# Seven block products for eight in nine more weight pairs, with one low part per pair made by an adding transfer

## The chip, the cores and the metric

The kernel runs on one core of a Trainium2 chip. A core has TensorE (PE in the profile; PEld is its weight load), VectorE (DVE), ScalarE (ACT), GpSimd (POOL) and SyncE (SP), an on-chip memory of 128 partitions, matrix accumulators in eight banks (PSUM), and 16 DMA engines that move data between HBM and the on-chip memory. The metric is the device time of one execution in microseconds.

## The reference

One encoder block over 256 positions of width 2048, in float32. What matters here are its five large matrix products: the input projection, the output projection `mix @ w_out` (2048 x 2048), the up product of the feed-forward part (2048 x 11264), its down product (5632 x 2048), and at the end a gate:

```
mix = jnp.concatenate([y_ssd, y_pool], axis=-1) @ w_out[i]
h = h + rmsnorm(mix, mix_norm_post[i])
hn = rmsnorm(h, ffn_norm_pre[i])
ff = conv_glu(hn, w_ffn_up[i], ffn_conv_w[i], ffn_conv_b[i], w_ffn_down[i])
h = h + rmsnorm(ff, ffn_norm_post[i])
gate = jax.nn.sigmoid(rmsnorm(h, ple_norm_pre[i]) @ w_ple_gate[i])
h = h + rmsnorm(gate * (p[i] @ w_ple[i]), ple_norm_post[i])
```

## The kernel before

**Products in three passes.** Every float32 operand is split into a high part, rounded to the format that PE multiplies in one pass, and a low part, the rest. A product is then three matmuls: high by high, high by low, low by high. `split` (L138) makes the two parts of a weight tile: ScalarE copies the tile with rounding (L147), VectorE subtracts the rounded copy from the tile (L148).

**Token-major products.** `token_major` (L240) computes 1024 columns of one product for both tiles of 128 positions. It is called twice per product, for half 0 and half 1 of the 2048 columns. The contraction runs over tiles of 128 (`k`), two at a time: a pair is one load of 2 x 128 rows by 1024 columns (1 MB, `raw`, L151, issued by SP, three buffers), and then the splits. The high and low parts live in five buffers each (tags `whi` and `wlo`), so a buffer is written again when PE has done with the tile five allocations before. A normal pair is 2 k x 2 position tiles x 2 column blocks x 3 passes = 24 matmuls of 128x512. In the last pair of a half the matmuls go bank by bank, so that the first banks can be emptied while the last are filled. In the second half of the gate the last four pairs go together in that way (`tail` is 4); eight of their tiles' high and low parts then have to be held at once, and two pairs get theirs in spare pages (`spare`, L136).

**Seven products for eight.** In the down product about one pair in three (`fast`) is not multiplied block by block. A pair is a 2 x 2 block product: two position tiles by two k tiles on one side, two k tiles by two column blocks on the other, eight block products. `seven_products` (L201) forms sums of the blocks on both sides and needs seven, 21 matmuls for 24. On the weight side VectorE makes the differences in place in the loaded pair (L209 to L211), and there are four splits: `a` (512 columns), `b`, `c` and `d` (1024 each). On the other side `hid_sums` (L800) makes four sums of 128x128 blocks, which are kept and used again in the second half. Four of the seven products go into accumulators of their own, and `combine` (L222) adds these to the four result banks after the last fast pair of the half, with VectorE, while the next pair runs.

**The order of the work.** The program's tile scheduler sets the order of each engine's queue when it is built; each engine then works through its queue in order and waits on semaphores. So an instruction that waits holds up everything behind it on its engine. In the output projection `sublayer` (L701) runs both halves, empties each bank with a square on ScalarE (L718) and a gain product on VectorE (L719), and then makes the next operand. The scan before it (`mix`, L604) ends in the same stretch of time as the projection begins, with additions on GpSimd (L612); the transposes of its result (`y_turn`, L686) run between pairs 2 and 4 of the projection. The gate's loop is at L864.

Of the kernel before, what the change touches and what calls it, by code (L numbers as in the profile page):

```python
# [16 lines left out]
P = 128  # L17
# [34 lines left out]
def build(nc, a, out):  # L52
# [5 lines left out]
    with tile.TileContext(nc) as tc, \  # L58
# [79 lines left out]
        def split(name, src, nel, cuts=()):  # L138
# [9 lines left out]
                last["dve"] = ins(nc.vector.tensor_sub(lo[:, s], src[:, s], hi[:, s].bitcast(F32)))  # L148
            return hi, lo

        def raw(name, src, a_, b_):  # L151
            r = wp.tile([P, 2048], F32, tag="raw", bufs=3, name=name)
            last["dma"] = load(r[:, :a_ * b_].rearrange("p (a b) -> p a b", a=a_), src, True)
            return r
# [43 lines left out]
                yield o, c  # L198
                c += o.shape[-1]

        def seven_products(name, r, a_, acc, alt, start, stop):  # L201

            v = r.rearrange("p (b c) -> p b c", b=4)
            b11 = split(f"{name}a", r[:, :512], 512)
            b2 = split(f"{name}b", r[:, 1024:], 1024)

            nc.vector.tensor_sub(v[:, 0:2], v[:, 1::2], v[:, 0:2])  # L209
            nc.vector.tensor_sub(v[:, 3], v[:, 3], v[:, 0])  # L210
            nc.vector.tensor_sub(v[:, 2], v[:, 2], v[:, 3])  # L211
# [10 lines left out]
        def combine(name, acc, alt):  # L222

            m = [mid(f"{name}v{i}") for i in range(2)]
            p1, s16, s165, s167 = (m[i // 2][:, i % 2 * 512:(i % 2 + 1) * 512] for i in range(4))

            def add(o, a_, b):
                nc.vector.tensor_add(o, a_, b)
# [11 lines left out]
        def token_major(name, w, c0, ks, get, acc, tail=1, fast=(), alt=None, sums=None):  # L240


            group, nu = [], len(ks) // 2
            for u in range(nu):
                k0 = ks[2 * u]
                r = raw(f"{name}r{k0}", w[k0 * P:(k0 + 2) * P, c0:c0 + 1024]
                        .rearrange("(k p) c -> p k c", p=P), 2, 1024)
                if u in fast:
                    seven_products(f"{name}{k0}", r, sums(k0), acc, alt, u == fast[0], u == fast[-1])
                    continue  # L250
                for j in range(2):
                    group.append((k0 + j, *split(f"{name}{k0}_{j}", r[:, j * 1024:(j + 1) * 1024], 1024)))
                if nu - tail <= u < nu - 1:
                    continue

                order = [(t, o, g, q) for t in range(2) for o in columns(acc[t]) for g in group for q in range(3)] \
                    if u == nu - 1 or u - 1 in fast[-1:] else \
                    [(t, o, g, q) for g in group for t in range(2) for q in range(3) for o in columns(acc[t])]
                for t, (o, c), (k, wh, wl), q in order:
                    xh, xl = (v[:, t * P:(t + 1) * P] for v in get(k))  # L260
                    xx, ww = ((xh, wh), (xh, wl), (xl, wh))[q]
                    mm(o, xx, ww[:, c:c + o.shape[-1]], k == ks[0] and q == 0, k == ks[-1] and q == 2)
                if u - 1 in fast[-1:]:
                    combine(name, acc, alt)
                group = []
                aside()

# [430 lines left out]
            load(g, src.partition_broadcast(P))  # L698
            return g

        def sublayer(name, w, ks, get, gain, h, vnext, panel=Panel, fast=((), ()), sums=None):  # L701

            mg = [page(f"{name}m{t}") for t in range(2)]
            sq = [[], []]
            for half in range(2):

                alt = main(f"{name}s{half}") if fast[half] and half == 0 else []
                acc = [main(f"{name}a{half}{t}") for t in range(2)]
                if fast[half]:
                    alt += (main(f"{name}s{half}") if half else []) + [misc(f"{name}s{half}_{i}") for i in (2, 3)]  # L710
                token_major(f"{name}{half}", w, half * 1024, ks, get, acc, 1, fast[half], alt, sums)
# [88 lines left out]
        def hid_sums(k):  # L800
# [3 lines left out]
            if k not in kept:  # L804
# [5 lines left out]
                s = mid(f"hd{k}")  # L810
                s1, s2, s3, s4 = (s[:, i * P:(i + 1) * P] for i in range(4))
                nc.vector.tensor_add(s1, a21, a22)
                nc.vector.tensor_sub(s3, a11, a21)
                nc.vector.tensor_sub(s2, s1, a11)
                nc.vector.tensor_sub(s4, a12, s2)
                o = keep[-1][:, n % 2 * 1024:(n % 2 + 1) * 1024] if n < 4 else mid(f"he{k}", F32R)
                nc.scalar.copy(o[:, :512], s[:, :512])
                nc.vector.tensor_sub(o[:, 512:], s[:, :512], o[:, :512].bitcast(F32))
                if n < 4:
                    kept[k] = o  # L820
            else:
                o = kept[k]
            d = {f"s{i + 1}": (o[:, i * P:(i + 1) * P], o[:, 512 + i * P:512 + (i + 1) * P]) for i in range(4)}
# [28 lines left out]
        def finish(t):  # L852
# [5 lines left out]
            for c in range(4):  # L858
# [2 lines left out]
                                               op0=ALU.mult, op1=ALU.add)  # L861
                nc.sync.dma_start(out[t * P:(t + 1) * P, s], vg[t][:, s])

        for half in range(2):  # L864
            acc = [main(f"gt{half}{t}") for t in range(2)]
            if half == 1:

                acc[1] = acc[1][:1] + [acc[1][1][:, :256], main("gtz")[0][:, :256]]

                for i in (8, 6):  # L870
                    sh, sl = page(f"gth{i}", F32R), page(f"gtl{i}", F32R)
                    for j in range(2):
                        spare[f"gt1{NK - i}_{j}"] = (sh[:, j * 1024:(j + 1) * 1024], sl[:, j * 1024:(j + 1) * 1024])
# [68 lines left out]
```

## Time and profile before

| what | us |
|---|---|
| median of 3 runs (1146.38 to 1147.10) | 1146.65 |
| the profiled execution | 1147.28 |
| its span | 1145.5 |
| PE busy in the span | 1126.3 |
| VectorE busy | 824.8 |
| ScalarE busy | 598.3 |
| GpSimd busy | 122.5 |

The profile is one execution. Busy time is the time in which an engine had an instruction at work; idle time of an engine that does not set the end costs nothing. The chain of work is followed back from the last instruction, at each step to what released it. PE's two edited stages are the output projection from 208.7 to 299.3 us and the gate product from 1042.4 to 1134.0 us of the span. A landing time of a transfer is from its issue to its semaphore.

### The profile page before, as it was taken

The page shows a single profiled execution, that of the slowest core. Times are in us where ns is not written, and L with a number is a line of the kernel's source. Part 1 is how long each engine was busy: PE and PEld are TensorE (multiplying, and loading weights), DVE is VectorE, ACT ScalarE, POOL GpSimd, SP SyncE. Part 2 cuts the span into 40 slices and gives each one's busy share as a digit, 9 for nine tenths or more (in the row PEclk, how much of TensorE's full clock was granted, in tenths as well). Part 3 has the DMA queues.
Part 4 walks back from the last instruction along what each step waited for, and adds up shares of the span by engine and source line. Part 5 has one row for each costly group of instructions (what it writes and reads, how often), then busy time and mean ns, then how long its engine had stood idle before and what let it go on. Part 6 is the DMA issues. An engine that isn't in the chain of part 4 may idle for free.

```text
span 1145.5 us, 15408 instructions
## 1 busy us (share of the span) xinstructions
PE 1126.3 (98%) x6057; PEld 971.6 (85%) x6057; DVE 824.8 (72%) x1060; ACT 598.3 (52%) x812; POOL 122.5 (11%) x123
## 2 busy tenths in 40 slices
PE   9998999999999999999999999999999999999996
PEld 9997987888888888888888888888888888887885
DVE  6578896654777665666766766668888888898573
ACT  7533543553675454544544545545555556657462
POOL 0274504200110000000000000000000000002001
PEclk9998999999999999999999999999999999999998
DMA  9952347546365555555555565556466646564752
GB/s 358 337 184 74 111 150 267 201 156 216 121 213 186 192 192 195 190 185 184 184 187 193 181 207 189 184 184 221 159 209 221 204 163 221 187 206 159 226 179 74
DMA packets 129592, 219.03 MB, mean 191 GB/s; under 512 B 3696, under 2 KB 96752, under 8 KB 128624
## 3 DMA queue, kind: packets, MB, share of 16 engines
q1 hardware_dynamic: 129232, 217.70, 57.4%
q8 instruction: 47, 0.77, 0.3%
q10 hardware_dynamic: 288, 0.36, 0.1%
q14 instruction: 25, 0.20, 0.1%
HBM read 215.95 MB, written 2.10 MB: 190 GB/s over the span
## 4 chain that ended last, share of the span: by engine, by line
PE 92%; DVE 5%; POOL 1%; ACT 1%; issue 1%; POOLq 0%; DVEq 0%; ACTq 0%
PE va L86 21%; PE ga L86 21%; PE dna L86 17%; PE woa L86 8%; PE gt L86 7%; PE dtu L86 4%; PE z L86 4%; PE xbc L86 3%; PE dns L86 3%; DVE cv L373 2%; DVE w L586 1%; DVE xb_0l L148 1%; PE ple L86 1%; PE yd L86 0%; DVE h L726 0%
## 5 line engine op out<-in xcount | busy, mean ns | idle before, releaser
L86 PE MATMUL ga<-wox,ug_0h 128*128 128x512 f32 x352 | 125.5, 395 | 0.0
L86 PE MATMUL ga<-wox,ug_1h 128*128 128x512 f32 x352 | 125.1, 394 | 0.0
L86 PE MATMUL va<-wox,uv_0h 128*128 128x512 f32 x352 | 124.8, 393 | 0.0
L86 PE MATMUL va<-wox,uv_1h 128*128 128x512 f32 x352 | 124.8, 393 | 0.0
L86 PE MATMUL ga<-wox,ug_0l 128*128 128x256 f32 x352 | 99.1, 282 | 0.0
L86 PE MATMUL ga<-wox,ug_1l 128*128 128x256 f32 x352 | 99.1, 282 | 0.0
L86 PE MATMUL va<-wox,uv_0l 128*128 128x256 f32 x352 | 99.1, 281 | 0.0
L86 PE MATMUL va<-wox,uv_1l 128*128 128x256 f32 x352 | 99.1, 281 | 0.0
L86 PEld LDWEIGHTS va<-wox,uv_0h 128*128 128x128 f32 x352 | 66.1, 188 | 15.0
L86 PEld LDWEIGHTS va<-wox,uv_1h 128*128 128x128 f32 x352 | 66.1, 188 | 15.0
L86 PEld LDWEIGHTS ga<-wox,ug_1h 128*128 128x128 f32 x352 | 66.1, 188 | 14.9
L86 PEld LDWEIGHTS ga<-wox,ug_0h 128*128 128x128 f32 x352 | 66.1, 188 | 14.8
L86 PE MATMUL dna<-dn_0h,hs 128*128 128x512 f32 x248 | 75.8, 393 | 0.0
L86 PE MATMUL dna<-dn_1h,hs 128*128 128x512 f32 x248 | 75.6, 393 | 0.0
L767 POOL TENSOR_TENSOR fc<-fc,rfb 128x1024 f32<-128x1024 f32 x11 | 26.4, 2404 | 440.2 <-ACT fc L766 440.2
L86 PEld LDWEIGHTS ga<-wox,ug_0l 128*128 128x128 f32 x352 | 66.2, 188 | 0.1
L86 PEld LDWEIGHTS ga<-wox,ug_1l 128*128 128x128 f32 x352 | 66.2, 188 | 0.0
L86 PEld LDWEIGHTS va<-wox,uv_0l 128*128 128x128 f32 x352 | 66.2, 188 | 0.0
L86 PEld LDWEIGHTS va<-wox,uv_1l 128*128 128x128 f32 x352 | 66.2, 188 | 0.0
L86 PEld LDWEIGHTS dna<-dn_1h,hs 128*128 128x128 f32 x248 | 46.5, 188 | 10.8
L86 PEld LDWEIGHTS dna<-dn_0h,hs 128*128 128x128 f32 x248 | 46.5, 188 | 10.7
L86 PE MATMUL dna<-dn_0l,hs 128*128 128x512 f32 x124 | 40.2, 393 | 0.0
(1075 smaller groups left out, 2860.3 us busy)
## 6 DMA issues: line engine op xcount, KB each, us to landing
dn0r<-w_ffn_down SPq DMA_DIRECT2D x22, 1024.0 KB, 5.5
dn1r<-w_ffn_down SPq DMA_DIRECT2D x22, 1024.0 KB, 5.5
zr<-w_in SPq DMA_DIRECT2D x8, 1024.0 KB, 5.2
wo0r<-w_out SPq DMA_DIRECT2D x8, 1024.0 KB, 5.6
wo1r<-w_out SPq DMA_DIRECT2D x8, 1024.0 KB, 5.5
gt0r<-w_ple_gate SPq DMA_DIRECT2D x8, 1024.0 KB, 6.0
gt1r<-w_ple_gate SPq DMA_DIRECT2D x8, 1024.0 KB, 5.6
dtur<-w_in SPq DMA_DIRECT2D x14, 528.0 KB, 8.6
```

The costliest lines, as they stand in the source:

```text
L86: nc.tensor.matmul(o, lhsT, rhs, start=start, stop=stop, skip_group_check=True)
L148: last["dve"] = ins(nc.vector.tensor_sub(lo[:, s], src[:, s], hi[:, s].bitcast(F32)))
L373: nc.vector.scalar_tensor_tensor(o[:, lo:hi], i[:, lo + d:hi + d], vec(wcol + j * wstep + f), o[:, lo:hi], op0=ALU.mult, op1=ALU.add)
L586: nc.vector.scalar_tensor_tensor(w[:, h * P:(h + 1) * P], cbm[:, 0, g, t, :], dt[:, t, 8 * g + h:8 * g + h + 1], w[:, h * P:(h + 1) * P], ...
L767: nc.gpsimd.tensor_tensor(cv.rearrange("p (f t) -> p f t", f=4), cv.rearrange("p (f t) -> p f t", f=4), rfb.unsqueeze(1).to_broadcast([P, ...
```

## The change

- Five pairs of the output projection (pair 5 of half 0; pairs 1, 2, 4 and 5 of half 1) and four of the gate product (pairs 3 and 5 of half 0; pairs 1 and 2 of half 1, with the pairs put in another order there) are done with seven block products. The sums on the position side are made by a new class `Sums` from the high and low parts of the operand, and kept for the second half.
- A new function `split_far` makes the low part in another way: ScalarE writes minus the rounded tile into the low buffer, GpSimd's queue issues a transfer that adds the same 512 KB of weights, read from HBM a second time, to what lies there, and ScalarE writes the high part. VectorE has no part in it. It is used for the second k tile of all 16 pairs of the output projection, of pairs 2 to 7 of the gate's half 0 and of all pairs of its half 1: 30 transfers. In a fast pair it makes the `b` parts.
- The two accumulators of 256 columns with which the gate's last bank ends now come in at `combine`, not at the start of the half. Two of the four extra accumulators are taken when the first fast pair comes, in the down product too.

```diff
+        def split_far(name, src, far, nel):
...
+            nc.scalar.activation(lo[:, :nel], src[:, :nel], AF.Copy, scale=-1.0)
+            o = lo[:, :nel]
...
+            nc.gpsimd.dma_start(o, far, accum_op=ALU.add)
+            nc.scalar.copy(hi[:, :nel], src[:, :nel])
+            return hi, lo
...
-            b2 = split(f"{name}b", r[:, 1024:], 1024)
+            b2 = split(f"{name}b", r[:, 1024:], 1024) if far is None else split_far(f"{name}b", r[:, 1024:], far, 1024)
...
+            if cut:
+                o = acc[1][1]
+                acc[1][1:] = [o[:, :256], alt[0][:, :256]]
+                add(acc[1][2], o[:, 256:], s165[:, 256:])
+                s165 = s165[:, :256]
             add(acc[1][1], acc[1][1], s165)
...
+                    if u == fast[0]:
+                        alt = alt + [misc(f"{name}s{i}") for i in (2, 3)]
...
-                    group.append((k0 + j, *split(f"{name}{k0}_{j}", r[:, j * 1024:(j + 1) * 1024], 1024)))
+                    k, s = k0 + j, r[:, j * 1024:(j + 1) * 1024]
+                    group.append((k, *(split_far(f"{name}{k0}_{j}", s, w[k * P:(k + 1) * P, c0:c0 + 1024], 1024)
+                                       if j and u in far else split(f"{name}{k0}_{j}", s, 1024))))
...
+        def pair_sums(name, s, o, a11, a21, a12, a22):
+
+            s1, s2, s3, s4 = (s[:, i * P:(i + 1) * P] for i in range(4))
+            nc.vector.tensor_add(s1, a21, a22)
+            nc.vector.tensor_sub(s3, a11, a21)
+            nc.vector.tensor_sub(s2, s1, a11)
+            nc.vector.tensor_sub(s4, a12, s2)
+            nc.scalar.copy(o[:, :512], s[:, :512])
+            nc.vector.tensor_sub(o[:, 512:], s[:, :512], o[:, :512].bitcast(F32))
...
+        class Sums:
...
+                    v = s[:, 512:]
+                    nc.vector.tensor_add(v, self.pan.hi[k // 8][:, c].bitcast(F32), self.pan.lo[k // 8][:, c].bitcast(F32))
+                    self.got[k] = pair_sums(...)
...
         hf = sublayer("wo", w_out, list(range(8, 16)) + list(range(8)), cat, gload("gmix", a["mix_norm_post"][0]), h,
-                      V_FN, Pairs)
+                      V_FN, Pairs, ((5,), (1, 2, 4, 5)), Sums("cs", cat), (range(8), range(8)))
...
+        hps = Sums("ps", hp)
         for half in range(2):
+            alt = [] if half else main(f"gts{half}")
             acc = [main(f"gt{half}{t}") for t in range(2)]
+            alt += main(f"gts{half}") if half else []
+            ks, fast = list(range(NK)), (3, 5)
             if half == 1:
-                acc[1] = acc[1][:1] + [acc[1][1][:, :256], main("gtz")[0][:, :256]]
-                for i in (8, 6):
+                ks, fast = [0, 1, 6, 7, 10, 11, 2, 3, 4, 5, 8, 9, 12, 13, 14, 15], (1, 2)
+                for i in (8, 10):
...
-            token_major(f"gt{half}", w_gate, half * 1024, list(range(NK)), hp, acc, 1 + 3 * half)
+            token_major(f"gt{half}", w_gate, half * 1024, ks, hp, acc, 1 + 3 * half, fast, alt, hps, range(2 - half * 2, 8))
```

More of the change, by code (lines that the diff above doesn't have):

```diff
@@ L149, in split @@
             return hi, lo
+        def split_far(name, src, far, nel):
+            if name in spare:
+                hi, lo = spare.pop(name)
+            else:
+                hi = wp.tile([P, 1056], F32R, tag="whi", bufs=5, name=f"{name}h")
+                lo = wp.tile([P, 1056], F32R, tag="wlo", bufs=5, name=f"{name}l")
+            nc.scalar.activation(lo[:, :nel], src[:, :nel], AF.Copy, scale=-1.0)
+            o = lo[:, :nel]
+            if len(far.shape) == 3:
+                o = o.rearrange("p (k c) -> p k c", k=far.shape[1])
+            nc.gpsimd.dma_start(o, far, accum_op=ALU.add)
+            nc.scalar.copy(hi[:, :nel], src[:, :nel])
+            return hi, lo
         def raw(name, src, a_, b_):
@@ L199, in columns, with seven_products @@
                 c += o.shape[-1]
-        def seven_products(name, r, a_, acc, alt, start, stop):
+        def seven_products(name, r, a_, acc, alt, start, stop, far):
             v = r.rearrange("p (b c) -> p b c", b=4)
             b11 = split(f"{name}a", r[:, :512], 512)
-            b2 = split(f"{name}b", r[:, 1024:], 1024)
+            b2 = split(f"{name}b", r[:, 1024:], 1024) if far is None else split_far(f"{name}b", r[:, 1024:], far, 1024)
             nc.vector.tensor_sub(v[:, 0:2], v[:, 1::2], v[:, 0:2])
@@ L237, in combine, with token_major @@
             add(s165, alt[2], s165)
+            if cut:
[3 more added lines that the diff above has]
+                s165 = s165[:, :256]
             add(acc[1][1], acc[1][1], s165)
-        def token_major(name, w, c0, ks, get, acc, tail=1, fast=(), alt=None, sums=None):
+        def token_major(name, w, c0, ks, get, acc, tail=1, fast=(), alt=None, sums=None,
+                        far=()):
             group, nu = [], len(ks) // 2
@@ L263, in token_major @@
                 if u - 1 in fast[-1:]:
-                    combine(name, acc, alt)
+                    combine(name, acc, alt, nu - tail == u + 1 and tail > 1)
                 group = []
@@ L699, in gload, with __init__, __call__, sublayer @@
             return g
-        def sublayer(name, w, ks, get, gain, h, vnext, panel=Panel, fast=((), ()), sums=None):
+        def pair_sums(name, s, o, a11, a21, a12, a22):
[6 more added lines that the diff above has]
+            nc.vector.tensor_sub(o[:, 512:], s[:, :512], o[:, :512].bitcast(F32))
+            return {f"s{i + 1}": (o[:, i * P:(i + 1) * P], o[:, 512 + i * P:512 + (i + 1) * P]) for i in range(4)}
+        class Sums:
+            def __init__(self, name, pan):
+                self.name, self.pan, self.pages, self.got = name, pan, [], {}
+            def __call__(self, k):
+                if k not in self.got:
+                    n = len(self.got)
+                    if n % 2 == 0:
+                        self.pages.append(page(f"{self.name}p{k}", F32R))
+                    s = mid(f"{self.name}s{k}")
+                    c = slice((k % 8) * L, (k % 8 + 2) * L)
+                    v = s[:, 512:]
+                    nc.vector.tensor_add(v, self.pan.hi[k // 8][:, c].bitcast(F32), self.pan.lo[k // 8][:, c].bitcast(F32))
+                    self.got[k] = pair_sums(f"{self.name}{k}", s, self.pages[-1][:, n % 2 * 1024:(n % 2 + 1) * 1024],
+                                            *(v[:, i * P:(i + 1) * P] for i in range(4)))
+                (h1, l1), (h2, l2) = self.pan(k), self.pan(k + 1)
+                return dict(self.got[k], a11=(h1[:, :P], l1[:, :P]), a12=(h2[:, :P], l2[:, :P]),
+                            a22=(h2[:, P:], l2[:, P:]))
+        def sublayer(name, w, ks, get, gain, h, vnext, panel=Panel, fast=((), ()), sums=None, far=((), ())):
             mg = [page(f"{name}m{t}") for t in range(2)]
@@ L709, in sublayer @@
                 if fast[half]:
-                    alt += (main(f"{name}s{half}") if half else []) + [misc(f"{name}s{half}_{i}") for i in (2, 3)]
-                token_major(f"{name}{half}", w, half * 1024, ks, get, acc, 1, fast[half], alt, sums)
+                    alt += main(f"{name}s{half}") if half else []
+                token_major(f"{name}{half}", w, half * 1024, ks, get, acc, 1, fast[half], alt, sums, far[half])
                 for t in range(2):
@@ L809, in hid_sums @@
                     keep.append(page(f"hsum{k}", F32R))
[L810 to L815, printed above, removed]
                 o = keep[-1][:, n % 2 * 1024:(n % 2 + 1) * 1024] if n < 4 else mid(f"he{k}", F32R)
-                nc.scalar.copy(o[:, :512], s[:, :512])
-                nc.vector.tensor_sub(o[:, 512:], s[:, :512], o[:, :512].bitcast(F32))
+                d = pair_sums(f"hd{k}", mid(f"hd{k}"), o, a11, a21, a12, a22)
                 if n < 4:
-                    kept[k] = o
+                    kept[k] = d
             else:
-                o = kept[k]
-            d = {f"s{i + 1}": (o[:, i * P:(i + 1) * P], o[:, 512 + i * P:512 + (i + 1) * P]) for i in range(4)}
+                d = dict(kept[k])
             d.update(a11=(h1[:, :P], l1[:, :P]), a12=(h2[:, :P], l2[:, :P]), a22=(h2[:, P:], l2[:, P:]))
```

7 lines of the change are left out of this document (4 added, 3 removed).

## The prediction

> **What bounds the kernel now.** I read the page first, then the busy time of the two stages that are edited, then the chain of work.
>
> ```profile
> PE 1126.3 (98%) x6057; PEld 971.6 (85%) x6057; DVE 824.8 (72%) x1060; ACT 598.3 (52%) x812; POOL 122.5 (11%) x123
> ...
> PE 92%; DVE 5%; POOL 1%; ACT 1%; issue 1%; POOLq 0%; DVEq 0%; ACTq 0%
> ```
>
> PE is 98% busy and is 92% of the chain, so time goes only where matmuls go or where PE is made to wait. The edited stages are the output projection (208.7 to 299.3 us) and the gate product (1042.4 to 1134.0):
>
> ```profile
> core 0: us, PE busy (x) PEld busy (x) DVE busy (x) ACT busy (x) POOL busy (x), PEclk, DMA share, GB/s
> 208.70:299.30 90.60, 90.60 (x402) 73.85 (x402) 50.09 (x55) 42.34 (x59) 7.17 (x17) 1.00 0.59 186
> 1042.40:1134.00 91.60, 89.36 (x436) 74.27 (x436) 57.11 (x67) 49.35 (x73) 5.03 (x14) 1.00 0.50 161
> ```
>
> In the projection PE never waits; in the gate it waits 2.2 us, at the start. VectorE and ScalarE are half busy, the DMA engines 0.50 to 0.59, the granted clock is 1.00. The chain, in order of time, gives the price of a matmul:
>
> ```profile
> 208.75 16.69 PE woa L86 x72
> ...
> 232.75 66.55 PE woa L86 x288
> ...
> 896.88 33.26 PE dna L86 x144
> ```
>
> 66.55/288 and 33.26/144 are both 0.231 us for a 128x512 matmul. A normal pair has 24, 5.54 us; a pair of seven products has 21, 4.85 us.
>
> **What is removed.** Nine pairs lose 3 matmuls each: 27 x 0.231 = 6.24 us, all on the chain. That the gate's second half has its 256-wide columns only from its fifth pair on I put at nothing: two of them are as many columns as the one that they replace. So 6.24 us is the most that can be gained.
>
> **What is added on VectorE and ScalarE.** The down product already has such pairs; a stretch of its VectorE row, start and length:
>
> ```profile
> 835.20 0.68 DVE L148 TENSOR_TENSOR dn016al<-dn0r,dn016ah 128x512 fp32r<-128x512 f32 x1
> 835.92 1.22 DVE L209 TENSOR_TENSOR dn0r<-dn0r 128x1024 f32<-128x1024 f32 x1
> 837.06 1.22 DVE L148 TENSOR_TENSOR dn016bl<-dn0r,dn016bh 128x1024 fp32r<-128x1024 f32 x1
> 838.31 0.69 DVE L210 TENSOR_TENSOR dn0r<-dn0r 128x512 f32<-128x512 f32 x1
> 839.04 0.69 DVE L211 TENSOR_TENSOR dn0r<-dn0r 128x512 f32<-128x512 f32 x1
> ...
> 840.33 1.23 DVE L148 TENSOR_TENSOR dn016cl<-dn0r,dn016ch 128x1024 fp32r<-128x1024 f32 x1
> 842.63 1.23 DVE L148 TENSOR_TENSOR dn016dl<-dn0r,dn016dh 128x1024 fp32r<-128x1024 f32 x1 [1.08 <-ACT dn016dh L147]
> ...
> 847.68 0.69 DVE L784 TENSOR_TENSOR hs<-hid,hs 128x512 fp32r<-128x512 f32 x1
> 848.28 1.22 DVE L148 TENSOR_TENSOR dn_0l<-dn0r,dn_0h 128x1024 fp32r<-128x1024 f32 x1
> ```
>
> The next starts 1.14 us after a 1024-wide one and 0.60 us after a 512-wide one (0.72 where it needs its result); I use 1.13, 0.60 and 0.65. Without the "b" split, which the adding transfer replaces, a fast pair asks VectorE for 0.6 + 1.13 + 0.65 + 0.65 + 1.13 + 1.13 = 5.3 us. Where its sums are new (three pairs of the projection, two of the gate) come 0.6 + 4 x 0.25 + 0.6 = 2.2 us, and after each half eight combining operations. The rows of a 128-wide sum and of a combining operation (the gain products have its size):
>
> ```profile
> L812 DVE TENSOR_TENSOR hd<-hid x9: 281/284/291, 771.0 to 919.1; 128x128 f32<-128x128 f32 x9
> ```
> ```profile
> L228 DVE TENSOR_TENSOR dna<-dna,dn0v x4: 692/693/696, 899.0 to 903.2; 128x512 f32<-128x512 f32 x4
> ```
>
> A far low part frees VectorE of 1.13 us and gives ScalarE one more activation, 0.95 us apart in the rows of the gate below; a fast pair is 4.8 us of ScalarE against 4.85 of PE. Over a stage both fit. In one place VectorE does not: half 1 of the projection, pairs 1 and 2, fast one behind the other. Call T0 the end of half 0's fast pair on PE. From T0 + 0.6 VectorE does, in its queue, 8 combining operations of 0.62 (5.0), a split 1.13, four gain products (2.5), pair 1 with sums (7.5), and of pair 2 the sums and the work up to the low part of its third block (5.5), with one sum of a later pair (0.6): 22.2 us, done at T0 + 22.8 if it never idles. In the fast pair above it waits for ScalarE's "d" copy for 1.08 us; with two such pairs and the wait for pair 2's "c" copy I put 2.7 on it, T0 + 25.5. PE asks for this part after half 0's last two pairs (11.1), pair 0 (5.54), pair 1 (4.85) and 7 matmuls: T0 + 23.1. The wait is between 0 and 2.4 us; I take 2.3, since the copies do queue behind subtractions. The other combining operations are covered by the next pair's 5.54 us or, at the end of the gate, by the last group.
>
> **The adding transfer** is new to this kernel: ScalarE writes minus the rounded half, GpSimd's queue issues a 512 KB transfer that adds the weights from HBM again, PE may start when it has landed. Call L the time from the end of ScalarE's negation to the landing. No row shows one. The nearest:
>
> ```profile
> wo1r<-w_out SPq DMA_DIRECT2D x8, 1024.0 KB, 5.5
> ...
> out<-vg SPq DMA_DIRECT2D x8, 256.0 KB, 2.7
> ```
>
> Between 256 KB in 2.7 and 1024 KB in 5.5 us, a plain 512 KB transfer would take 3.6 us: the low end. If the engines must read the destination as well, they move 1024 KB, 5.5 us, and with about 1 us for GpSimd, whose small steps take 0.3 us and its additions 2.2 in the rows below, 6.5: the high end. I take 5.0, the middle, because at 0.59 busy the engines are shared with the 1 MB loads.
>
> What L costs depends on how early the negation can run. There are five pairs of tiles for high and low parts, so a low part is rewritten only when PE is done with the tile five allocations before. Worked out once, for pair 6 of half 0, behind the fast pair: the tile was the fast pair's first block's, released after 3 of its 21 matmuls; ScalarE then has to copy a high part and negate (2 x 0.95), done 2.0 us before the fast pair ends; in PE's queue the low part is first used 8 matmuls (1.85 us) into pair 6. L may be 3.8. In the same way, by the queues of the built program: half 1 pair 2, 5.0 (PE is already held by VectorE); pair 3, 3.1 (its negation stands behind pair 2's late copies); pair 5, 3.8; gate half 1 pair 2 and half 0 pair 6, 3.9 each; gate half 0 pair 2, 4.1. Its negation comes after two long squares and two small copies, where a copy starts now at 1057.66, and ends at 1058.7; PE is there 16 matmuls into the pair, at 1062.8, counted back from the end of the first bank of pair 7 (1088.2, 6 matmuls and 5 pairs earlier is the pair's start):
>
> ```profile
> 1055.05 1.98 ACT L338 ACTIVATE rpj<-h 128x2048 f32<-128x2048 f32 x1
> 1056.85 0.26 ACT L338 ACTIVATION_READ_ACCUMULATOR rpj<-h 128x1 f32 x1
> 1056.94 0.90 ACT L183 ACTIVATE dnxh<-dnxt,vt 128x256 fp32r<-128x256 f32 x2
> 1057.66 1.13 ACT L147 CAST gt_1h<-gt0r 128x1024 fp32r<-128x1024 f32 x1
> 1058.59 1.14 ACT L147 CAST gt_0h<-gt0r 128x1024 fp32r<-128x1024 f32 x1
> ...
> 1088.25 0.69 ACT L885 ACTIVATE gth<-gt,rh 128x512 f32<-128x512 f32 x1 [0.39 <-PE gt L86]
> ```
>
> Elsewhere between normal pairs 11 us pass from release to use, and L is hidden whatever it is in this range. Sum of what exceeds the seven budgets: L = 3.6, 0.5 us; 4, 1.5; 5, 1.2 + 0 + 1.9 + 1.2 + 1.1 + 1.1 + 0.9 = 7.4; 6.5, 17.9.
>
> The Trainium skill (DMA: Bandwidth & Descriptors, Anatomy of one DMA — SWDGE (gpsimd) path) fits a transfer issued from GpSimd with 2.0 us plus bytes/436e3; for 524,288 bytes that is an estimate of 3.2 us, and the sum by it would be 6.24 - 2.3 - 0.1, 3.8 us faster. No run here shows a transfer from GpSimd, and the page does not price the adding.
>
> **GpSimd's queue.** The first adding transfers stand between the steps that finish the scan, on which PE waits there, and the third behind the row norm:
>
> ```profile
> 196.54 2.19 POOL L612 TENSOR_TENSOR y<-y,ym 128x512 f32<-128x512 f32 x1 [5.69 <-DVE ym L610]
> ...
> 217.73 0.29 POOL L680 TENSOR_SCALAR yn1r<-yn1r,rz 128x2 f32<-128x2 f32 x1
> ```
>
> ```profile
> 192.13 1.05 ACT L147 CAST wo_1h<-wo0r 128x1024 fp32r<-128x1024 f32 x1 [4.39 <-PE z L86]
> ```
>
> GpSimd idled 5.69 us ahead of the first of these, and the negation, which takes the place of the copy at 192.13, ends about 3.5 us before it: hidden while GpSimd holds the transfer for less than 3.5 us. The third can be issued only at 218.0, and PE wants it 62 matmuls after 208.75, at 223.1: a budget of 5.1 from there, 0 at L = 5. SP issues no more than before.
>
> **Sum.** Against the profiled execution, 1147.28 us, which is 0.63 above the median of the runs: - 6.24 + 2.3 + 7.4 = + 3.5, 1150.8; against the median 1150.1, rounded to 1150. The break-even is L = 4.4.
>
> **Rivals.** *Faster*: the transfer lands in 3.6 to 4 us, as the small plain ones suggest. Then 0.5 to 1.5 us of waits remain, and 2.3 or less on VectorE: - 6.24 + 2.3 + 0.5 = - 3.4, about 1143; with no VectorE wait 1141. It decides at L = 4.4, and against it speaks that reading the destination is work the plain rows do not have. *The DMA engines fill up*: a pair now moves 1.5 MB, or 2 MB if the destination read counts. The projection's 0.59 x 90.6 = 53.5 us of engine time moves 186/0.59 = 315 GB/s when busy; 16 transfers of 0.52 MB add 27 us (0.91 of 88 us) or, doubled, 53 us: 107 us where PE has 87, 16 us longer than before. The gate's 45.8 + 23 or 47 us ends at 69 or 92, about 5 longer with its uneven loads. That gives about 1168. The Trainium skill (DMA: Bandwidth & Descriptors, Issuing engines are not separate DMA queues) says that all queues run on the same 16 engines, which is how this rival would work; no run here shows two queues loaded at once. *No difference*: L between 4.0 and 4.8 puts the sum within 2.3 us of zero, 0.2%, which is about what a measurement of this kernel can tell from no change.
>
> **How the numbers follow.** Slower by waits, 0.45, 1150, its own range 1149 to 1160; faster, 0.34, 1143; within 0.2%, 0.10; engines full, 0.11, 1168. Slower in all 0.56. The range 1141.5 to 1164 leaves out the far end of the last and the best of the second, under 2 in 10.
>
> **What would show it.** Right: the 512 KB issues from GpSimd landing at 5 us or more, PE idle ahead of matmuls on a low part with a DMA named, once in each of the pairs listed, and one wait on VectorE in half 1 pair 2; no wait between normal pairs. The faster rival: landing below 4 us and PE full in both windows. The third: DMA share near 1 and plain 1 MB loads far above 5.5 us. The prediction is wrong if L is outside 4.4 to 6, or if the queue of copies on ScalarE runs further ahead than I worked out.

## The result: 1208.18 us, 5.4% slower

The changed kernel takes 1208.18 us (median of 1204.97 to 1212.39) beside 1146.66 us: a ratio of 1.054, with a 95% interval of 1.050 to 1.058. The forecast was 1150, with a range to 1164.

The head of its page, the busy time of the engines and the chain's shares by engine:

```profile
PE 1144.5 (95%) x6006; PEld 979.6 (81%) x6006; DVE 860.4 (71%) x1144; ACT 644.6 (53%) x870; POOL 149.6 (12%) x153
...
PE 79%; DMA 10%; DVE 6%; issue 3%; ACT 2%; POOL 1%; POOLq 0%; DVEq 0%; ACTq 0%
```

TensorE was 92% of the chain and is 79%; DMA, which had no share before, is 10%, most of it the adding transfers. TensorE has fewer matmuls (6006 rows for 6057) and yet is busy for 18 us longer: it has run part of them slowly. The two stages, from first matmul to last, after (the projection, then the gate product; the columns are length, busy time of each engine, granted clock, DMA share, GB/s):

```profile
208.30:330.40 122.10, 99.23 (x388) 78.14 (x388) 71.54 (x105) 65.84 (x90) 18.83 (x31) 0.90 0.76 193
1074.80:1201.70 126.90, 102.23 (x421) 81.42 (x420) 72.71 (x104) 71.27 (x101) 18.11 (x30) 0.88 0.68 174
```

and before, cut the same way (the gate product's last matmul ends at 1136.8, not at 1134.0):

```profile
208.60:299.30 90.70, 90.70 (x403) 73.95 (x403) 50.09 (x55) 42.34 (x59) 7.27 (x17) 1.00 0.59 186
1042.50:1136.80 94.30, 92.01 (x457) 76.77 (x455) 57.86 (x69) 50.23 (x75) 5.84 (x16) 1.00 0.49 156
```

The projection is 31.4 us longer and the gate product 32.6; the span is 65.1 longer in all (1210.6 for 1145.5; the profiled execution, 1212.39 us, is the longest of the four, so this is 3.6 more than the medians show). Two things show in each row. Length less PE busy time, the idle time, is 22.9 and 24.7 us where it was 0 and 2.3. And PE busy time went up though matmuls went away: 99.2 where 90.7 less 15 x 0.231 makes 87.2, and 102.2 where 92.0 less 12 x 0.231 makes 89.2; the granted clock is 0.90 and 0.88. Together:

| Term | forecast, us | measured, us |
|---|---|---|
| 27 matmuls removed | -6.24 | -6.24 |
| VectorE's wait in half 1, pair 2 | +2.3 | 0 |
| waits on adding transfers | +7.4 | +45.3 |
| matmuls at a lower clock | not foreseen | +25.0 (12.0 and 13.0) |
| outside the two stages | 0 | +1.1 |
| sum | +3.5 | +65.1 |

The -6.24 in the last column is 27 times 0.231, the row on the clock is the rest of PE's busy time in the two stages, and the row below it the rest of the span.

What TensorE waited for, after (in all, times, longest):

```profile
PE gt L86 <- DMA gt_1l<-w_ple_gate: 20.6, 6, 5.5
PE woa L86 <- DMA wo_1l<-w_out: 19.8, 5, 6.0
...
PE woa L86 <- DMA wo112bl<-w_out: 1.9, 1, 1.9
PE gt L86 <- DMA gt110bl<-w_ple_gate: 1.8, 1, 1.8
PE woa L86 <- DMA wo12bl<-w_out: 1.2, 1, 1.2
```

All fourteen waits that are new are on adding transfers, 45.3 us; eleven of them are on a normal pair's low part (`_1l`), three on a fast pair's (`bl`). The DMA issues of the projection tell why (in all, KB each, median us from issue to landing):

```profile
wo1r<-w_out SPq DMA_DIRECT2D x8, 1024.0 KB, 6.7
wo0r<-w_out SPq DMA_DIRECT2D x7, 1024.0 KB, 7.1
wo_1l<-w_out POOLq DMA_DIRECT2D x11, 512.0 KB, 9.6
...
wo02bl<-w_out POOLq DMA_DIRECT2D x1, 512.0 KB, 5.5
wo110bl<-w_out POOLq DMA_DIRECT2D x1, 512.0 KB, 7.9
wo112bl<-w_out POOLq DMA_DIRECT2D x1, 512.0 KB, 5.5
```

A fast pair's adding transfer that hardly meets a load lands after 5.5 us (four of the nine; the other five take 6.9 to 11.0); a normal pair's takes 9.6 in the median. The moment at which one of these is issued, in the timeline:

```profile
244.71 1.06 ACT L158 ACTIVATE wo_1l<-wo0r 128x1024 fp32r<-128x1024 f32 x1
...
245.79 0.37 SPq L118 DMA_DIRECT2D wo1r<-w_out  x1
...
246.06 0.86 POOL L162 DMA_DIRECT2D wo_1l<-w_out  x1 [10.74 <-PE wo0s L86]
```

The scheduler placed ScalarE's negation behind the rounded copy of the same block, so it is the last reader of the raw buffer. Its end at 245.77 releases two transfers: SyncE's next 1 MB load, 0.02 us later, and the adding transfer, 0.29 us later. The load is issued first and lands at 251.89, the transfer at 255.31. In eleven of the 21 normal pairs with such a transfer the negation's end releases a load in this way; nine of the eleven normal transfers that TensorE waits for are among them. TensorE comes for this low part at 249.4 and gets it at 255.35, and what follows is seen in steps of 1 us (columns as above):

```profile
253.00:254.00 1.00, 0.00 (x0) 0.00 (x0) 0.00 (x0) 0.00 (x0) 0.00 (x0) 1.00 0.94 233
254.00:255.00 1.00, 0.00 (x0) 0.00 (x0) 0.00 (x0) 0.00 (x0) 0.00 (x0) 0.56 1.06 287
255.00:256.00 1.00, 0.65 (x2) 0.55 (x3) 0.00 (x0) 0.00 (x0) 0.00 (x0) 0.50 1.04 279
...
259.00:260.00 1.00, 1.00 (x4) 0.81 (x3) 0.00 (x0) 0.00 (x0) 0.00 (x0) 0.50 0.11 45
...
261.00:262.00 1.00, 1.00 (x6) 0.80 (x5) 1.00 (x2) 0.78 (x1) 0.00 (x0) 1.00 0.00 0
```

The DMA engines are full (0.94 to 1.06) while PE idles; towards the end of the wait the granted clock drops to 0.50, and PE runs at it until 261, its matmuls 0.43 us apart in place of 0.23. The trace's clock records have eleven such stretches in the two stages, each 3.4 or 6.8 us long, 54.6 us in all.

### The profile page after: what moved, and what is told of

Read it like the earlier page. It is cut to its first block, busy times and chain, and to the rows that moved or that the text cites. A ratio compares the mean times of both kernels' runs of the same rounds, so it can differ in the third digit from the quotient of the medians.

```text
span 1210.6 us, 15564 instructions
## 1 busy us (share of the span) xinstructions
PE 1144.5 (95%) x6006; PEld 979.6 (81%) x6006; DVE 860.4 (71%) x1144; ACT 644.6 (53%) x870; POOL 149.6 (12%) x153
## 3 DMA queue, kind: packets, MB, share of 16 engines
q1 hardware_dynamic: 129232, 217.70, 54.4%
q0 software_dynamic: 4320, 15.73, 7.0%
## 4 chain that ended last, share of the span: by engine, by line
PE 79%; DMA 10%; DVE 6%; issue 3%; ACT 2%; POOL 1%; POOLq 0%; DVEq 0%; ACTq 0%
PE va L86 20%; PE ga L86 20%; PE dna L86 16%; DMA wo_1l<-w_out 4%; PE woa L86 4%; PE z L86 4%; DMA gt_1l<-w_ple_gate 3%; PE dtu L86 3%; PE gt L86 3%; PE xbc L86 3%; DVE cv L400 2%; DMA gt1r<-w_ple_gate 2%; PE dns L86 1%; PE dn1s L86 1%; DVE h L785 1%
## 5 line engine op out<-in xcount | busy, mean ns | idle before, releaser
L86 PE MATMUL ga<-wox,ug_1l 128*128 128x256 f32 x352 | 99.2, 282 | 0.7 <-DVE ug_1l L148 0.7
L86 PE MATMUL ga<-wox,ug_0l 128*128 128x256 f32 x352 | 99.2, 282 | 0.0
L86 PEld LDWEIGHTS dna<-dn_1h,hs 128*128 128x128 f32 x248 | 46.5, 188 | 10.8
L86 PEld LDWEIGHTS dna<-dn_0h,hs 128*128 128x128 f32 x248 | 46.5, 188 | 10.7
L86 PE MATMUL gt<-gt_1l,dnxh 128*128 128x512 f32 (+1 forms) x40 | 18.6, 511 | 22.9 <-DMA gt_1l<-w_ple_gate 20.6
```

What stands on the lines that cost most here:

```text
L86: nc.tensor.matmul(o, lhsT, rhs, start=start, stop=stop, skip_group_check=True)
```

## The experiments

Theory at the start: a transfer is late because it stands behind the 1 MB load that its own negation releases, and each wait costs a halved clock on top. Rivals: adding is slow by itself, or the fast pairs' own work is late. Durations of stages below are cut from the first matmul of the stage to its last, as above.

**No adding transfer.**

```diff
         def split_far(name, src, far, nel):
-
+            return split(name, src, nel)
```

> The changed kernel with its nine pairs of seven products, but no adding transfer: every low part is the subtraction on VectorE again. Theory: all of the loss comes from the adding transfers (their landing 9 to 10 us after the issue, and the halved clock behind each wait), so without them the 6.24 us of matmuls are gained, less some waits on VectorE where two fast pairs stand one behind the other (2 to 5 us): 1142 to 1145 us, no granted clock below 1.00 in the two stages. Rival: the seven products themselves are late (VectorE, ScalarE), the transfer only makes it visible: 1160 us or more.

1159.18 us, ratio 1.010 (1.009 to 1.012). Four fifths of the loss is gone, but the kernel is still 12 us slower than before, which the theory did not expect and the rival did. Its projection, and three of its new waits:

```profile
207.70:301.70 94.00, 90.61 (x389) 71.62 (x388) 82.93 (x116) 50.57 (x71) 6.06 (x11) 0.98 0.53 165
...
PE ga L86 <- DVE ug_0l L148: 2.5, 1, 2.5
...
PE wos L86 <- ACT wo112ch L147: 1.7, 1, 1.7
...
PE woa L86 <- ACT wo112dh L147: 0.9, 1, 0.9
```

VectorE is busy for 82.9 of 94.0 us. PE waits 3.4 us here and again behind the projection, for VectorE, whose last addition to `h` starts 10.7 us after the projection's last matmul (9.0 before): from the last matmul of the projection to the first on `va` it takes 40.2 us where it took 32.7, with PE idle for 5.8 of it (0.6 before). In each of the two stretches the clock is halved once, for 3.4 us, which the theory had ruled out for the projection. The projection costs 3.3, the stretch behind it 7.5, the gate product 0.8. So nine pairs of seven products lose by themselves, as the rival had it; that the transfers only make this visible does not hold, since the other four fifths of the loss went with them.

**The load held back until the transfer has landed.** In normal pairs a one-column addition on GpSimd reads raw weights and finished low part:

```diff
             nc.scalar.copy(hi[:, :nel], src[:, :nel])
+            if name[-1] == "1": nc.gpsimd.tensor_add(tiny(f"{name}w", 1), lo[:, :1].bitcast(F32), src[:, :1])
             return hi, lo
```

> The changed kernel; in normal pairs a one-column addition on GpSimd reads the raw weights and the finished low part, so that the raw buffer, and with it the next 1 MB load, is released only when the adding transfer has landed. Theory: an adding transfer takes 5.4 us alone and 9 to 10 behind a 1 MB load that the same negation releases; with the load held back each lands after 5.4 to 5.7, the seven budgets of the prediction are exceeded by 12 us in all, few waits are long enough for the halved clock (3 us): 1156 us (1150 to 1165). Rival: the addition itself is slow whatever else moves: landing stays at 9 us, 1205 us or more.

1206.66 us, ratio 1.051 (1.050 to 1.053): no gain, and the theory's 1156 falls. Its waits:

```profile
PE woa L86 <- DMA wo_1l<-w_out: 10.8, 4, 5.0
PE woa L86 <- DMA wo110bl<-w_out: 6.6, 1, 6.6
PE gt L86 <- DMA gt06bl<-w_ple_gate: 5.5, 1, 5.5
...
PE woa L86 <- DMA wo12bl<-w_out: 4.9, 1, 4.9
PE gt L86 <- DMA gt_1l<-w_ple_gate: 4.7, 3, 2.1
```

The waits on normal pairs went down (19.8 to 10.8 in the projection, 20.6 to 9.0 in the gate product with 4.3 on its spare tiles, the medians of their landings from 9.6 to 7.0 and from 9.1 to 5.5), but those on the fast pairs' transfers went from 4.9 to 23.7 us. For this the run has two causes that it does not separate. The delayed loads now meet these transfers: five of the nine land after 8.5 to 9.5 us. And GpSimd works through its queue in order, so that the added instruction, while it waits for a landing, holds up the next issue:

```profile
272.85 0.54 POOL L164 TENSOR_TENSOR wo_1w<-wo_1l,wo1r 128x1 f32<-128x1 f32 x1 [8.36 <-DMA wo_1l<-w_out]
273.33 0.87 POOL L162 DMA_DIRECT2D wo110bl<-w_out  x1
```

ScalarE's negation for `wo110bl` had ended at 268.45, 4.9 us before this issue; at `wo02bl` and `gt06bl` it is 2.7 and 2.5 us. So what holding the load back is worth by itself stays open.

**A plain transfer in place of the adding one** (the subtraction of the rounded half is left out of the result).

```diff
-            nc.gpsimd.dma_start(o, far, accum_op=ALU.add)
+            nc.gpsimd.dma_start(o, far.bitcast(F32R))
```

> The changed kernel, its transfer a plain one: the low part becomes the weights themselves, so the subtraction of the rounded half is left out of the result. Same bytes, same queues, same waits. Theory: the 4 KB packets go from 0.33 us to 0.16, which takes 1.4 us off a landing, but it still stands behind the 1 MB load: 8 us, waits of 28 us and some 17 us of halved clock, 1186 us (1175 to 1195). Rival: the adding is what is slow; a plain transfer lands in 3.6 to 5 us, 1145 to 1155 us.

1184.24 us, ratio 1.032 (1.030 to 1.034), as the theory had it. Same bytes, same queue, same order (an issue holds GpSimd for 0.53 us in place of 0.86): landings of a fast pair's transfer take 4.0 us where nothing disturbs them, those of normal pairs 7.2:

```profile
PE woa L86 <- DMA wo_1l<-w_out: 13.1, 5, 3.7
PE gt L86 <- DMA gt_1l<-w_ple_gate: 10.3, 5, 3.8
```

Adding is therefore worth 24 us of the 61.5, and the rival's "only the adding" is out: a plain transfer is late too.

**Negation ahead of the rounded copy**, so that the copy releases the load:

```diff
-            nc.scalar.activation(lo[:, :nel], src[:, :nel], AF.Copy, scale=-1.0)
+            neg = ins(nc.scalar.activation(lo[:, :nel], src[:, :nel], AF.Copy, scale=-1.0))
...
-            nc.scalar.copy(hi[:, :nel], src[:, :nel])
+            with tc.issue_after(neg): nc.scalar.copy(hi[:, :nel], src[:, :nel])
```

> The changed kernel, ScalarE's negation put ahead of the rounded copy of the same block, so that the negation isn't the last reader of the raw buffer: the 1 MB load is released about 0.7 us after the adding transfer instead of 0.27 us ahead of it, and the negation itself is 0.95 us earlier. Theory: the two share the engines instead of standing one behind the other, landing 6 to 7 us after the issue, 14 us of waits and 5 of halved clock: 1160 us (1153 to 1172). Rival, the order of the two doesn't matter: only 0.95 us less at each of the ten or eleven waits, 1195 us.

1194.99 us, ratio 1.042 (1.041 to 1.044): the rival's number. Normal pairs' transfers of the projection land after 10.3 us, no sooner; those of the gate product after 6.8, where it was 9.1. The transfer shown above, now ahead of its load, lands after 6.6 us in place of 9.3, but the next one, behind that load, after 10.4 in place of 10.0. So the order matters for single transfers, which the rival denied, but it does not remove the lateness.

With these four the theory changes: not the order alone but the demand on the DMA engines. Share times length gives the engine time of the projection: 0.59 x 90.7 = 53.5 us before, 0.53 x 94.0 = 49.8 with nine fast pairs and no extra transfer, 0.76 x 122.1 = 92.8 in the changed kernel. Sixteen adding transfers take 43 us, 2.7 each; PE has 87.2 us of matmuls there. The next runs test it.

**Adding transfers in fast pairs alone.**

```diff
-                                       if j and u in far else split(f"{name}{k0}_{j}", s, 1024))))
+                                       if False else split(f"{name}{k0}_{j}", s, 1024))))
```

> The changed kernel with an adding transfer only in the nine fast pairs; normal pairs split on VectorE. In a fast pair the raw buffer is released by later work, so no load is released together with the transfer. Theory (a transfer is late because a 1 MB load stands ahead of it): each lands after 5.4 us, waits of 1 to 2 us at three or four places, VectorE has 9 x 1.13 us less to do than with all splits, which was 1159: 1157 us (1153 to 1162), no more halved clock than with all splits. Rival (the addition is slow by itself): landing at 9 us, waits of 5 us in most fast pairs, 1180 us or more.

1168.35 us, ratio 1.019 (1.017 to 1.020): 9 us more than with no such transfer, and 11 above the theory. Six of nine land after 5.5 to 5.7 us, the other three, issued 1.4 to 2.0 us behind a 1 MB load, after 7.1 (`wo112bl`), 7.4 (`gt06bl`) and 7.9 (`gt110bl`); PE waits longest for these three:

```profile
PE gt L86 <- DMA gt110bl<-w_ple_gate: 3.6, 1, 3.6
PE gt L86 <- DMA gt06bl<-w_ple_gate: 3.2, 1, 3.2
PE woa L86 <- DMA wo112bl<-w_out: 3.1, 1, 3.1
```

In place of 1.13 us of VectorE comes a transfer of 5.5 or more, for a part that PE uses early in its pair. Of the six that landed early, PE still waited for three, 1.1 to 1.8 us.

**Adding transfers without any fast pair**, in the kernel before:

```diff
-                    group.append((k0 + j, *split(f"{name}{k0}_{j}", r[:, j * 1024:(j + 1) * 1024], 1024)))
+                    group.append((k0 + j, *(split_far(f"{name}{k0}_{j}", r[:, j * 1024:(j + 1) * 1024], w[(k0 + j) * P:(k0 + j + 1) * P, c0:c0 + 1024], 1024) if j and u in far else split(f"{name}{k0}_{j}", r[:, j * 1024:(j + 1) * 1024], 1024))))
```

> The kernel before, with all its eight products, and the adding transfers of the changed kernel in the projection's and the gate product's pairs. Theory: a transfer lands 9 to 10 us after the issue here too, since its negation releases a 1 MB load, but between normal pairs 11 us pass from the release of a tile to its use, so most of it is hidden: 1149 us (1146 to 1155); the loss of the changed kernel needs both, late copies of fast pairs and late transfers. Rival: with 1.5 MB per pair, and the destination read, the engines are asked for more than a pair's 5.54 us; waits build up in both stages without any fast pair, 1175 us or more.

1172.77 us, ratio 1.022 (1.021 to 1.024), 25.6 us more than before: 2 us short of the rival's bound and far above the theory's 1155. "Hidden between normal pairs" does not hold. The two stages:

```profile
208.10:305.00 96.90, 92.96 (x403) 75.10 (x403) 33.52 (x41) 55.66 (x74) 18.34 (x32) 0.98 0.93 255
1048.00:1162.80 114.80, 100.11 (x457) 81.31 (x455) 41.91 (x55) 63.49 (x89) 17.49 (x30) 0.93 0.71 192
```

In the projection the engines are 0.93 busy, 90 us, and the stage is 6.2 us longer. Most of this is one wait of 2.6 us with 3.4 us at half clock behind it, on the third transfer, which is issued at 216.3 beside the scan's last steps; of the other fifteen PE waits for one, 1.3 us. The gate product is 20.5 longer, 12.4 of it waits on `gt_1l`.

**The same in every second pair** (the difference is to the kernel just above).

```diff
-                token_major(f"{name}{half}", w, half * 1024, ks, get, acc, 1, fast[half], alt, sums, range(8) if name == "wo" else ())
+                token_major(f"{name}{half}", w, half * 1024, ks, get, acc, 1, fast[half], alt, sums, range(1, 8, 2) if name == "wo" else ())
...
-            token_major(f"gt{half}", w_gate, half * 1024, list(range(NK)), hp, acc, 1 + 3 * half, far=range(2 - half * 2, 8))
+            token_major(f"gt{half}", w_gate, half * 1024, list(range(NK)), hp, acc, 1 + 3 * half, far=range(3 - half * 2, 8, 2))
```

> The kernel before, all eight products, with an adding transfer in every second pair only (15 transfers where every pair had 30 and the time was 25.6 us longer). Theory: it is the demand on the DMA engines that costs: 0.59 busy without transfers and 0.93 with all in the projection, so half of them makes 0.76 and the waits nearly vanish: 1151 us (1148 to 1155). Rival: each transfer has a price of its own (issue, latency), half of them cost half: 1160 us or more.

1160.16 us, ratio 1.011 (1.010 to 1.013). In all it is the rival's number, but not by the rival's way:

```profile
207.90:298.70 90.80, 90.80 (x404) 74.01 (x403) 41.79 (x48) 49.09 (x67) 13.37 (x25) 1.00 0.80 231
1041.80:1148.00 106.20, 95.81 (x457) 78.92 (x455) 49.75 (x62) 56.74 (x82) 11.44 (x23) 0.97 0.59 173
```

In the projection eight adding transfers cost nothing at all: PE never waits, at 0.80. There the price is not one per transfer. At which share of the engines it begins is not shown, since the transfer on which most of the loss at 0.93 fell is not among these eight. In the gate product half of the transfers cost 11.9 us, with the engines 0.59 busy over the stage. Two waits make 8.1 us of it; the longer, 4.5, falls where the engines are 0.83 busy, right after the row norm (1058 to 1073). So the demand over a stage does not explain the gate product; there it is a matter of a few bad moments.

**Fewer loads beside the transfers.** Sixteen of the 32 loads of 1 MB are left out: the normal pairs split an earlier pair's raw block, so their high parts are not of their own weights.

```diff
-                r = raw(f"{name}r{k0}", w[k0 * P:(k0 + 2) * P, c0:c0 + 1024]
-                        .rearrange("(k p) c -> p k c", p=P), 2, 1024)
+                if u in fast or u == 0 or (len(fast) > 1 and "wo1" in name and u in (3, 6)) or (name == "gt1" and u == 3):
+                    r = raw(f"{name}r{k0}", w[k0 * P:(k0 + 2) * P, c0:c0 + 1024].rearrange("(k p) c -> p k c", p=P), 2, 1024)
+                    kept_r = kept_r if u in fast else r
...
+                r = kept_r
```

> The changed kernel without most 1 MB loads of normal pairs in the two stages: they split the raw block that an earlier normal pair loaded (left out: their own weights in the high parts). The adding transfers are all there. Theory: with no load released by the negation a transfer lands after 5.4 us, within 2 us of the prediction's budgets; the waits of the first halves shrink to 2 us each, those of the second halves, which still load half of their pairs, by less: 1168 us (1155 to 1180). Rival: the transfer is slow by itself, 1200 us or more.

1179.53 us, ratio 1.028 (1.027 to 1.030): at the upper end of the theory's range. The landings of normal pairs are 6.9 and 5.8 us (9.6 and 9.1), the waits on adding transfers 24.8 us (45.3). Half of the loads removed, 45% of the waits gone; what is left are transfers that meet a remaining load, or the adding transfer before them, and budgets that 5.5 us exceeds.

**PE kept busy during the waits**, with matmuls of a zero operand:

```diff
+                    n = FILL.get((name, u), 0) if k % 2 and q == 1 else 0
+                    for i in range(n):
+                        with tc.issue_after(lastmm):
+                            lastmm = mm(o, zero, wh[:, c:c + 512], False, False)
```

> The changed kernel with 95 matmuls of a zero stationary operand (they add nothing) put into PE's queue ahead of the five waits of the projection on a normal pair's low part: 12, 30, 13, 18 and 22, 21.9 us of work in place of the idle time. Theory: the clock is halved by the idle time itself, so with PE busy it stays at 1.00 there; the stage gets shorter by half of its 23.9 us at halved clock, though it does 21.9 us more: 1198 us (1194 to 1203). Rival: the halving comes from something else (transfers, load of the memory), or it costs nothing because the transfers would be late anyway: 1206 us or more.

1203.15 us, ratio 1.049 (1.047 to 1.051). Its projection:

```profile
209.00:324.90 115.90, 111.62 (x484) 89.88 (x483) 73.56 (x106) 65.53 (x90) 19.71 (x32) 0.99 0.81 211
```

Although 21.9 us of matmuls were added, the stage is 6.2 us shorter, with the clock at 0.99 for 0.90 and 3.4 us at half clock for 23.9. So the idle time is what halves the clock, and the halving does cost time. But only 6 of the 10 us expected came back: idle and filler together are 26.2 us where 22.9 were idle. A PE that runs faster asks for the next transfer sooner, and waits for it.

**Five fast pairs, spread, and no adding transfer.**

```diff
-                      V_FN, Pairs, ((5,), (1, 2, 4, 5)), Sums("cs", cat), (range(8), range(8)))
+                      V_FN, Pairs, ((3,), (1, 3)), Sums("cs", cat))
...
-            ks, fast = list(range(NK)), (3, 5)
+            ks, fast = list(range(NK)), (3,)
...
-                ks, fast = [0, 1, 6, 7, 10, 11, 2, 3, 4, 5, 8, 9, 12, 13, 14, 15], (1, 2)
+                ks, fast = [0, 1, 10, 11, 6, 7, 2, 3, 4, 5, 8, 9, 12, 13, 14, 15], (2,)
...
-            token_major(f"gt{half}", w_gate, half * 1024, ks, hp, acc, 1 + 3 * half, fast, alt, hps, range(2 - half * 2, 8))
+            token_major(f"gt{half}", w_gate, half * 1024, ks, hp, acc, 1 + 3 * half, fast, alt, hps)
```

> No adding transfer, and five pairs of seven products instead of nine: one (the fourth pair) in the first half of the projection, the second and fourth in its second half, one in each half of the gate product; no two stand one behind the other and none near the end of the projection. Theory: with all nine it was 12 us slower because VectorE falls behind where two stand one behind the other (waits of 3 us) and is late for the norm after the projection (7 us); spread out, the 15 matmuls (3.5 us) are gained nearly whole: 1144.5 us (1143 to 1147). Rival: one fast pair alone already costs VectorE more than its 0.69 us on PE, no gain: 1147 to 1152 us.

1146.35 us beside 1147.37, ratio 0.9987 (0.9978 to 0.9996): faster by 1 us, 0.1%, which the interval only just tells from no change; still the only version below the kernel before. Fifteen matmuls are 3.5 us; a third of it arrived. One stretch of 3.4 us at half clock at the start of the gate product, which the profile of the kernel before does not have, cost 1.7.

## Why the prediction was wrong

**What bounds, what is removed.** Right: time goes only where TensorE is made to wait, and in the sum the 6.24 us stand. That the later 256-wide columns are worth nothing holds as well: 48 matmuls 0.119 us apart became 24 of 0.231, 0.2 us.

**VectorE.** The 2.3 us in half 1, pair 2 did not show: PE had been held by transfers before it came there. Without them it was close: in the kernel with no adding transfer PE waits 1.7 and 0.9 us in that pair, named as waits on ScalarE's copies, which queue behind VectorE's subtractions, as the step said. What that step missed stood elsewhere: the stretch behind the projection, in which PE waits for VectorE and which is 7.5 us longer in that kernel.

**The adding transfer: the step that failed.** It took L as 5.0, 6.5 at most. Issue to landing is 9.6 and 9.1 us in the median, with 0.3 from the negation's end to the issue. For a transfer alone the estimate was close (5.5 and 0.3). The step said that the engines are shared with the 1 MB loads, but added only a middle value for it, and did not ask what else the negation's end releases: in half of the normal pairs a load of twice the bytes, at the same moment. The budgets were not what failed. With the L that each of its seven places had (5.7 to 9.9 us) they give 25.4 us in all, and 23.7 were measured there. The other 21.6 us stand outside them: 2.8 at the third transfer, for which there was a budget of 5.1 and which took 9.1, and 18.8 at six pairs that were taken as hidden, with "11 us from release to use". From the negation's end to the use it was 5.5 to 7.5 us there, enough for L = 5.0; at five of the six L was 9.7 to 10.8.

**Rival "the DMA engines fill up"**, with a chance of 0.11, held the mechanism: engine time nearly doubled (that reading the destination is the reason is not shown by a run), 107 us of demand in the projection (measured 92.8) and 92 in the gate product (0.68 x 126.9 = 86.3). Its price, 1168, was far too low: it compared totals over a stage, and transfers that bunch cost waits long before a stage is full, as the gate product with every second transfer shows; and it had no clock in it. That transfers and fast pairs together cost 61.5 where each alone costs 25.6 and 12.1 fits with this: a fast pair leaves less time between release and use. This is argued; no run takes it apart further.

**The term that was missing**: the clock. 25.0 us of the 65.1 are matmuls at half clock behind waits. The prediction quoted a granted clock of 1.00 and carried it through every case. The Trainium skill (TensorE: Matmul & The Clock Gate, What's actually happening) has the rule: the array's clock is halved after an idle window of about 3.4 us, counted in windows that run freely, and comes back after a busy one. The lengths of 3.4 and 6.8 us agree with it, and so does where the stretches begin: in each trace on one grid of 3.41 us (here 226.82, 254.12, 274.60 and 298.50 are 8, 6 and 7 steps apart). How much idle time it takes differs: less than a whole window was enough.

In this kernel waits of 2.3 to 3.4 us were already followed by half clock, those of 1.9, 1.8 and 1.2 were not. What decides is the idle time within one step of the grid, not the length of the wait: the eleven steps before a stretch held 2.24 to 3.41 us of it, and of the steps without a stretch behind them none held more than 1.37. In all twelve traces the clock was halved after every step with 1.9 us or more and after none with 1.8 or less. Between these two both occur: a step with 1.84 us was followed by half clock (in the run with zero matmuls, at 1170.4), one with 1.88 was not (in the run without adding transfers, at 1059). A wait of 3.2 us that the grid divided into 1.65 and 1.55 was not followed by it either (transfers in fast pairs alone, ending at 1082). The wait of 2.2 us at the start of the gate product is in both kernels; here 2.24 us of it lie in one step, before it was divided into 1.73 and 0.51.

The zero matmuls show that, of such a loss, some comes back as waiting once the clock is kept.

## What to carry to other kernels

When a new transfer is priced, look up what else the event that starts it also releases, and add up engine time in that moment, not over the stage; a transfer that lands in 5.5 us alone took 9.6 beside loads twice its size. A wait of TensorE that can fill 1.9 us of one 3.41 us step is to be priced with the slow matmuls behind it, here half as much again over all waits. And before a subtraction of 1.1 us is replaced by a transfer, compare it with the time from release to use, not with the load of the engine that it frees.

## What the runs showed that was not expected

An adding transfer takes nearly twice the engine time per byte of a plain one. In the changed kernel's table of queues q0, which carries them alone, moved 15.73 MB in 7.0% of 16 engines' span and q1, the loads, 217.70 MB in 54.4%:

```profile
q1 hardware_dynamic: 129232, 217.70, 54.4%
q0 software_dynamic: 4320, 15.73, 7.0%
```

Per MB that is 5.4 us of the span of 1210.6 us for 3.0. With the plain transfers from the same queue the row is

```profile
q0 software_dynamic: 4320, 15.73, 4.0%
```

and makes 3.0 as well, of a span of 1182.6 us: the adding is the difference, not the queue. The Trainium skill (DMA: Bandwidth & Descriptors, Rules for kernel authors) says that an accumulating transfer reads its destination and writes it later, which agrees; it gives no price. And eight of them in the projection were free, with the engines 0.80 busy; of sixteen, at 0.93, PE waited for two, 3.9 us in all.
